# One driver for every seven-product unit, with weights prepared two pairs of products ahead

## The chip, the cores and the metric

One Trainium2 chip, one core. The metric is the device time of one execution in microseconds; the median of three runs is given, and one further execution is profiled. TensorE (PE) multiplies matrices, ScalarE (ACT) and VectorE (DVE) work elementwise, GpSimd (POOL) and SyncE (SP) mainly issue transfers here.

## The reference

One layer of a streaming encoder over 1024 tokens of width 1024, with 256 memory tokens, all in float32:

```python
h = rms_norm(x, g_mix)
c_h, c_b, c_c, sq, sk, sv, xq, gate_pre = split(h @ w_in)
y_conv = (c_b * causal_depthwise_conv(c_c * c_h, conv_w)) @ w_conv_out      # width 3
y_sb = stick_breaking_attention(heads(sq), heads(sk), heads(sv)) @ w_sb_out  # 16 heads of 64
mem_n = rms_norm(mem, g_mem)
y_x = memory_cross_attention(xq, mem_n, w_mem_kv, q_norm_g, k_norm_g) @ w_x_out  # 4 heads of 256
g = sigmoid(gate_pre)                                                        # one gate per branch
x = x + (g[0] * y_conv + g[1] * y_sb + g[2] * y_x) @ w_out
x = x + square(relu(rms_norm(x, g_mlp) @ w_up)) @ w_down                     # w_up 1024x4096
```

## The kernel before

TensorE multiplies fp32r operands. To keep float32 accuracy each operand is split in a rounded part (hi) and the rest (lo), and a product is three matmuls, hi*hi, hi*lo and lo*hi, for each of the pieces of 128 rows that it sums over. A *split* is one ACT instruction, which writes hi, and one DVE instruction behind it, which writes lo = source - hi (`split_o`).

Large products are done by a scheme that makes a 2x2 block product from seven half-size products instead of eight. One *unit* (class `Unit`) takes two column blocks of weights of 512 KB each (`load` fills `r1` and `r2`) and makes four 128x512 tiles per block pair. Its seven products are `p1` to `p7`; each is a `chain_mm` of twelve 128x512 matmuls into a PSUM bank. Its weights come in four steps: `w1` splits r1; `w2` and `w3` do two DVE subtractions or additions of half blocks and split the result; `w4` splits half of r2. `p1` and `p2` need w1, `p6` and `p5` need w2, `p7` and `p3` need w3, and `p4` needs w4. Bank `a` serves p1, p6, p7 and p4 one after the other, and is read out in between: after p1 into `x0`, after p6 into `xu` (ACT), after p7 (DVE), after p4 (ACT). A product that goes on in a bank waits for that reading. `fin` is what follows a unit.

The other operand are halves of the normed rows and their sums and differences, made once for a group of units by class `Seconds`: `first` makes those for p1 and p2; `second_a(rows, kk)`, for kk = 0 to 3, does eight transposes on TensorE, two evictions on ACT, four half-wide DVE instructions and a split, for p6 and p5; `second_b(kk)` does two splits, for p7, p3 and p4.

`drive(U, extra)` runs a list of units. It is called twice. *Drive 1* (from about 94 us to 373 us) has 13 units: four `QUnit`, and then three groups of an `HUnit`, a `CUnit` and a `BUnit`. The `fin` of a CUnit multiplies C by H on DVE and applies the three taps of the convolution: for each of two tiles one ACT instruction (the first tap) and two DVE instructions (the others). The `fin` of a BUnit multiplies the result by B and stores it. *Drive 2* (1625 us to 1957 us) has 16 `FUnit`, the w_up product. Between the drives stand the attention, the gates and the output products; behind drive 2 stands the w_down product, whose weights are fetched by `fetch(n)` and prepared by `prep(n, kp)`.

Ahead of drive 1, and before the change outside of it, eight products of the memory rows are made, `kv(0)` to `kv(7)`, 256 columns each, of 48 matmuls with 128x256 results; their weights come by `kv_load` and are split by `kv_split` (a CAST on ACT, a subtraction on DVE). kv(4) to kv(7) are interleaved with second_a(0) to second_a(3) of drive 1.

What sets the order: `act`, `vec` and the first matmul of each chain_mm are recorded by `keep_in_program_order`, so that these instructions stand on their engines as the code issues them; the other instructions are placed by a scheduler. Each engine works its row off in order. Pools give the buffers: 4 raw pages for loaded weights, 3 `whl` pages for split ones, 40 general pages, 3 pages for x0, and PSUM banks: 3 in `pd` (units' bank a), 2 in `pz`, 2 for transposes, 1 in `po`.

Of the kernel before, what the change touches and what calls it, by code (L numbers as in the profile page):

```python
# [42 lines left out]
def block_kernel(ctx, tc, x, mem, small, w_in, w_v, w_kv, w_co, w_so, w_xo, w_out, w_up, w_dn, out):  # L43
# [199 lines left out]

    def split_o(src, hi, lo):
        act(hi, src)
        vec(lo, src, ALU.subtract, f32v(hi))
# [13 lines left out]
    def chain_mm(ps, a, b, first=False, last=False):  # L260

        n = len(a)
        for i, ((ah, al), (bh, bl)) in enumerate(zip(a, b)):
            go = dict(skip_group_check=not first)
            m_ = nc.tensor.matmul(ps, lhsT=ah, rhs=bh, start=first and i == 0, stop=False, **go)  # L265
            if i == 0:
                order(m_)
            nc.tensor.matmul(ps, lhsT=ah, rhs=bl, start=False, stop=False, **go)  # L268
            nc.tensor.matmul(ps, lhsT=al, rhs=bh, start=False, stop=i == n - 1, **go)  # L269
# [52 lines left out]
    class Unit:  # L322
# [30 lines left out]

        def half(self):
            return hpp.tile([P, 512], F32, tag="hp", name=nm("xh"))

        def p1(self):
            self.a, self.x0 = pd(), self.half()
            chain_mm(self.a, col4(self.a11), self.h["11"], first=True)
            act(self.x0, self.a)  # L360
# [49 lines left out]
    def drive(U, extra):  # L410


        extra = iter(extra)

        def ex():
            next(extra, lambda: None)()

        NU = len(U)
        U[0].load()
        U[1].load()  # L420
        U[0].w1()
        U[1].w1()
        for u in range(2):
            ex()
            U[u].p1()
            ex()
            U[u].p2()
            U[u].w2()
        for u in range(2):
            ex()  # L430
            U[u].p6()
            ex()
            U[u].p5()
        for u in range(NU):
            un = U[u]
            nx = U[u + 1] if u + 1 < NU else None
            if u == 0:
                un.w3()
            if u < 2:
                un.w4()  # L440
            else:
                un.p1()
                U[u - 1].fin()
                un.w3()
                un.p2()
                un.w4()
            if u + 2 < NU:
                U[u + 2].load()
            if u >= 2:
                un.p6()  # L450
                un.p5()
            if u >= 1 and nx:
                nx.w1()
            un.p7()
            if u == 0:
                nx.w3()
            elif nx:
                nx.w2()
            un.p3()
            un.p4()  # L460
            if u == 0:
                un.fin()
        U[NU - 1].fin()
# [20 lines left out]
    def kv(cg):  # L484
# [3 lines left out]
        for i in range(NM):  # L488
            ps = pd()[:, 0:256]
# [51 lines left out]
    kv_load(5)  # L541
# [4 lines left out]
    for kk in range(4):  # L546
        kv_split(4 + kk)
        steps = kv(4 + kk)
        fill(steps, 4)
        if kk + 6 < 8:  # L550
            kv_load(kk + 6)
        sec_h.second_a(rows1, kk)
        run(steps)
    for i in range(NM):
        nc.gpsimd.dma_start(out=kv_scr[1][i], in_=vr[i])
    pin[0] = False
# [67 lines left out]
    drive(units, [lambda kk=kk: sec_h.second_b(kk) for kk in range(4)])  # L624
# [6 lines left out]
    for kk in range(4):  # L631
# [4 lines left out]
        split_o(h12[kk // 2][:, j * 512 : j * 512 + 512], *sec_h.h["12"][kk])  # L636

# [461 lines left out]
    class FUnit(Unit):  # L1099
# [36 lines left out]
    drive(  # L1136
        [FUnit(u) for u in range(16)],
        [lambda kk=kk: sec_f.second_a(late, kk) for kk in range(4)]
        + [lambda kk=kk: sec_f.second_b(kk) for kk in range(4)],
    )  # L1140
# [32 lines left out]
    def prep(n, kp):  # L1173
# [5 lines left out]
        t_ = tt.get((q, kp))  # L1179
        if j == 1:  # L1180
# [11 lines left out]
    fetch(0)  # L1192
    fetch(1)
    prep(0, 0)
    prep(0, 1)
# [84 lines left out]
```

## Time and profile before

| | before |
|---|---|
| median of 3 runs | 2268.62 us (2268.49 to 2269.18) |
| the profiled execution | 2269.87 us |
| its span | 2268.1 us |
| mean granted TensorE clock | 0.984 |
| DMA, mean over the span | 116 GB/s, 263.94 MB |

Rows of the timeline read: start and duration in us, engine, line of the code, operation, output<-input by the program's names, shape, how many instructions in a row are put together (x2), and in brackets the idle time of the engine ahead of it with what released it. In rows of time windows each engine has its busy time and, in parentheses, its number of instructions; behind them stand the granted clock (1 is full), the share of time in which the DMA engines were busy, and GB/s. Matmuls overlap, so the duration of one (0.39) is longer than the time from one start to the next (0.23). Names in capital L are lines: L236 is `act`, L233 is `vec`, L89 and L90 are the cast and the subtraction of the kv weights, L265, L268 and L269 the three matmuls of chain_mm, L203 to L205 those of kv, L603 the taps on DVE, L284 the eviction of transposes.

### The profile page before, as it was taken

How to read it: one execution, taken by the hardware profiler on the slowest of the kernel's cores; microseconds unless marked ns; L12 is line 12 of the kernel's file. 1: busy time of each engine (PE TensorE's matmuls, PEld its weight loads, DVE VectorE, ACT ScalarE, POOL GpSimd, SP SyncE). 2: the span in 40 equal slices, each digit the busy share in tenths (PEclk: the TensorE clock that was granted, in tenths of full speed). 3: DMA queues.
4: the chain of work that ended last, by engine and by line, in shares of the span. 5: the costliest groups of instructions: out<-in, count | busy, mean ns of one | idle time of the engine just before them, and what ended most of it. 6: DMA issues, size and time to landing. Idle time of an engine off the chain costs nothing.

```text
span 2268.1 us, 27004 instructions
## 1 busy us (share of the span) xinstructions
PE 2174.7 (96%) x10148; PEld 1800.8 (79%) x10148; DVE 1406.0 (62%) x1885; ACT 1004.3 (44%) x1791; POOL 385.1 (17%) x570
## 2 busy tenths in 40 slices
PE   6899998999999999999999999999989999999999
PEld 6778776888878778778788788888768888788887
DVE  4745555145688788787777534442565555677776
ACT  7522323235565565566555312111455555433332
POOL 1000000112333433433333000000111111100000
PEclk9999998999999999999999999999989999999999
DMA  5341224323222222222221445334134444744444
GB/s 205 130 130 56 75 74 162 94 88 112 84 75 66 84 80 69 75 84 65 75 93 66 140 142 163 105 100 151 68 120 154 152 150 152 264 174 135 153 149 139
DMA packets 74883, 263.94 MB, mean 116 GB/s; under 512 B 9728, under 2 KB 9728, under 8 KB 74752
## 3 DMA queue, kind: packets, MB, share of 16 engines
q1 hardware_dynamic: 53248, 188.27, 25.7%
q0 software_dynamic: 21504, 73.94, 8.7%
q8 instruction: 80, 1.31, 0.2%
q14 instruction: 51, 0.42, 0.1%
HBM read 179.86 MB, written 73.92 MB: 112 GB/s over the span
## 4 chain that ended last, share of the span: by engine, by line
PE 71%; DVE 10%; issue 7%; ACT 7%; POOL 4%; DMA 1%; POOLq 0%; DVEq 0%; ACTq 0%; SPq 0%
PE d L204 7%; PE d L205 6%; PE d L203 6%; PE d L269 6%; PE d L265 6%; PE d L268 6%; PE d L125 4%; PE d L126 4%; PE d L127 4%; PE z L265 4%; PE z L269 4%; PE z L268 4%; POOL pg L836 3%; DVE pg L233 2%; DVE pg L114 2%
## 5 line engine op out<-in xcount | busy, mean ns | idle before, releaser
L203 PE MATMUL d<-pg,whl 128*128 128x512 f32 x736 | 294.6, 400 | 0.3 <-ACT ox L744 0.3
L204 PE MATMUL d<-pg,whl 128*128 128x512 f32 x736 | 288.0, 391 | 0.0
L205 PE MATMUL d<-pg,whl 128*128 128x512 f32 x736 | 287.8, 391 | 0.0
L236 ACT ACTIVATE pg<-pg 128x512 f32<-128x512 f32 (+1 forms) x192 | 150.9, 791 | 305.6 <-DVE pg L233 303.6
L233 DVE TENSOR_TENSOR pg<-pg,pg 128x1024 fp32r<-128x1024 f32 (+3 forms) x180 | 184.7, 1032 | 72.2 <-ACT pg L236 70.4
L836 POOL TENSOR_SCALAR_AFFINE_SELECT pg<-pg 128x128 f32<-128x128 f32 x256 | 171.2, 675 | 279.6 <-ACT pg L833 269.2
L846 DVE TENSOR_TENSOR_SCAN pg<-pg,zero 128x128 f32<-128x128 f32 (+7 forms) x128 | 177.1, 1384 | 57.1 <-POOL pg L836 54.4
L265 PE MATMUL d<-pg,whl 128*128 128x512 f32 x444 | 179.6, 404 | 29.3 <-ACT pg L236 17.7
L113 ACT CAST pg<-t 128x256 fp32r<-128x256 f32 (+2 forms) x336 | 115.2, 368 | 203.0 <-DVE pg L114 145.4
L269 PE MATMUL d<-pg,whl 128*128 128x512 f32 x444 | 178.8, 403 | 2.5 <-DVE whl L233 2.4
L268 PE MATMUL d<-pg,whl 128*128 128x512 f32 x444 | 178.4, 402 | 1.2 <-DVE pg L233 1.2
L205 PEld LDWEIGHTS d<-pg,whl 128*128 128x128 f32 x736 | 138.2, 188 | 30.7
L203 PEld LDWEIGHTS d<-pg,whl 128*128 128x128 f32 x736 | 138.4, 188 | 25.8 <-ACT ox L744 1.1
L204 PEld LDWEIGHTS d<-pg,whl 128*128 128x128 f32 x736 | 138.6, 188 | 24.4
L265 PE MATMUL z<-pg,whl 128*128 128x512 f32 x396 | 154.9, 391 | 0.0
L269 PE MATMUL z<-pg,whl 128*128 128x512 f32 x396 | 154.6, 390 | 0.0
L268 PE MATMUL z<-pg,whl 128*128 128x512 f32 x396 | 154.6, 390 | 0.0
L125 PE MATMUL d<-pg,whl 128*128 128x512 f32 x384 | 150.7, 393 | 3.0 <-ACT whl L89 3.0
L89 ACT CAST whl<-raw 128x1024 fp32r<-128x1024 f32 x78 | 82.6, 1059 | 158.7 <-DMA raw<-in_w_co 62.8
L126 PE MATMUL d<-pg,whl 128*128 128x512 f32 x384 | 150.5, 392 | 0.0
L127 PE MATMUL d<-pg,whl 128*128 128x512 f32 x384 | 149.9, 391 | 0.0
L114 DVE TENSOR_TENSOR pg<-t,pg 128x256 fp32r<-128x256 f32 (+2 forms) x336 | 129.3, 404 | 30.5 <-ACT pg L113 27.1
(192 smaller groups left out, 4754.6 us busy)
## 6 DMA issues: line engine op xcount, KB each, us to landing
raw<-in_w_in SPq DMA_DIRECT2D x72, 512.0 KB, 3.6
raw<-in_w_up SPq DMA_DIRECT2D x32, 512.0 KB, 4.3
raw<-fscr_s SPq DMA_DIRECT2D x32, 512.0 KB, 3.7
pg<-in_w_dn SPq DMA_DIRECT2D x32, 512.0 KB, 4.9
gscr<-pg POOLq DMA_DIRECT2D x24, 512.0 KB, 2.9
raw<-gscr SPq DMA_DIRECT2D x24, 512.0 KB, 3.9
fscr<-pg POOLq DMA_DIRECT2D x48, 256.0 KB, 2.6
fscr_s<-pg POOLq DMA_DIRECT2D x48, 256.0 KB, 2.5
```

Of the source, the lines that this page charges most:

```text
L125: nc.tensor.matmul(ps, lhsT=ah, rhs=bh, start=i == 0, stop=False)
L126: nc.tensor.matmul(ps, lhsT=ah, rhs=bl, start=False, stop=False)
L127: nc.tensor.matmul(ps, lhsT=al, rhs=bh, start=False, stop=i == n - 1)
L203: nc.tensor.matmul(ps, lhsT=ah, rhs=bh, start=i == 0, stop=False)
L204: nc.tensor.matmul(ps, lhsT=ah, rhs=bl, start=False, stop=False)
L205: nc.tensor.matmul(ps, lhsT=al, rhs=bh, start=False, stop=i == n - 1)
L233: order(nc.vector.tensor_tensor(out=out, in0=a, in1=b, op=op))
L265: m_ = nc.tensor.matmul(ps, lhsT=ah, rhs=bh, start=first and i == 0, stop=False, **go)
L268: nc.tensor.matmul(ps, lhsT=ah, rhs=bl, start=False, stop=False, **go)
L269: nc.tensor.matmul(ps, lhsT=al, rhs=bh, start=False, stop=i == n - 1, **go)
L836: nc.gpsimd.affine_select(out=t_[:, W - P : W], in_=t_[:, W - P : W], pattern=[[-1, P]], compare_op=ALU.is_gt, fill=fill_, base=0, channel ...
L846: nc.vector.tensor_tensor_scan(out=rev, data0=rev, data1=zero.broadcast_to([P, W]), initial=1.0, op0=ALU.mult, op1=ALU.add)
```

## The change

1. `split_o` issues the DVE half of a split later: behind the next split's ACT half, or ahead of the next chain_mm (`owed`, `settle`).
2. `drive` goes through one list of pairs of products: (1, u) is p1 and p2 of unit u, (2, u) is p6 and p5, (3, u) is p7, p3 and then p4. It begins with (1,0) (1,1) (1,2) (1,3) (2,0) (2,1) (3,0) (3,1) (2,2) (3,2) (2,3) (3,3), and from unit 4 on has (1,u) (2,u) (3,u). Before, units 0 and 1 were interleaved, and from unit 2 on each went alone. Behind the first product of a pair the weights for the pair after the next are prepared. w4 and the load of unit u + 2 come in the pair ahead of (3, u). A unit's `fin` comes behind the second product of the next pair; before, it came behind p1 of the next unit, ahead of w3 and p2.
3. The four first units' r1 are loaded ahead, and once more by the later `load` (eight more loads of 512 KB in both drives). Unit 3 uses the bank of `po`.
4. In drive 1 kv(4) stays ahead of the drive; second_a(0) and kv(5), second_a(1), second_a(2) and kv(6), second_a(3), kv(7) are hooked in behind p2(0), p1(1), p2(1), p1(2), p2(2). The kv products use `pz` banks in place of `pd`. second_b(0) to (3) are hooked behind p6 and p5 of units 0 and 1.
5. In drive 2 second_a(0) to (3) come behind p2(0), p1(1), p2(1), p1(2), and second_b as in drive 1.
6. The last unit of drive 2 has the first fetches of w_down ahead of its p7, and the two first preparations ahead of its p3 and p4; before, all came behind the drive.

```diff
+    owed = []
+    def settle():
+        while owed:
+            lo, src, hi = owed.pop(0)
+            vec(lo, src, ALU.subtract, f32v(hi))
     def split_o(src, hi, lo):
         act(hi, src)
-        vec(lo, src, ALU.subtract, f32v(hi))
+        settle()
+        owed.append((lo, src, hi))
...
     def chain_mm(ps, a, b, first=False, last=False):
         n = len(a)
+        settle()
...
+        bank = staticmethod(pd)
         def p1(self):
-            self.a, self.x0 = pd(), self.half()
+            self.a, self.x0 = self.bank(), self.half()
...
-    def drive(U, extra):
+    def drive(U, hooks, late=None):
...
+        pairs = [(1, u) for u in range(4)] + [(2, 0), (2, 1), (3, 0), (3, 1)]
+        for u in range(2, NU):
+            pairs += [(k, u) for k in ((1, 2, 3) if u >= 4 else (2, 3))]
+        def prep(n):
+            if n < len(pairs):
+                k, u = pairs[n]
+                getattr(U[u], f"w{k}")()
+        for u in range(4):
+            U[u].r1 = load(U[u].s1_)
+        for n in range(2):
+            prep(n)
+        hook(-1, 0)
+        U[3].bank = po
+        done = None
+        for n, (k, u) in enumerate(pairs):
             un = U[u]
+            first, second = ((un.p1, un.p2), (un.p6, un.p5), (un.p7, un.p3))[k - 1]
+            final = n == len(pairs) - 1
+            if final and late:
+                late(0)
+            first()
+            prep(n + 2)
+            if n == 1:
+                U[0].load()
+            if n + 1 < len(pairs) and pairs[n + 1][0] == 3:
+                v = pairs[n + 1][1]
+                U[v].w4()
+                if v + 2 < NU:
+                    U[v + 2].load()
+            hook(n, 0)
+            if n == 2:
+                U[1].load()
+            if final and late:
+                late(1)
+            second()
+            if done:
+                done.fin()
+                done = None
+            hook(n, 1)
+            if k == 3:
+                if final and late:
+                    late(2)
+                un.p4()
+                done = un
+        done.fin()
...
-            ps = pd()[:, 0:256]
+            ps = pz()[:, 0:256]
...
-    for kk in range(4):
-        kv_split(4 + kk)
-        steps = kv(4 + kk)
-        fill(steps, 4)
-        if kk + 6 < 8:
-            kv_load(kk + 6)
-        sec_h.second_a(rows1, kk)
-        run(steps)
+    kv_split(4)
+    run(kv(4))
...
-    drive(units, [lambda kk=kk: sec_h.second_b(kk) for kk in range(4)])
+    hooks = {(-1, 0): lambda: kv_load(5), (0, 1): a_(0, 5), (1, 0): a_(1), (1, 1): a_(2, 6), (2, 0): a_(3), (2, 1): lambda: kv_late(7)}
+    hooks.update({(4 + kk // 2, kk % 2): b_(sec_h, kk) for kk in range(4)})
+    drive(units, hooks)
...
-    fetch(0)
-    fetch(1)
-    prep(0, 0)
-    prep(0, 1)
+    def ahead(i):
+        if i == 0:
+            fetch(0)
+            fetch(1)
+        else:
+            prep(0, i - 1)
+    drive([FUnit(u) for u in range(16)], hooks, ahead)
```

Three places show what this moves. The first is ACT's row where drive 1 begins. Before, around kv(4) and kv(5): whl_628 and pg_631 are kv(4)'s casts, t_666 and t_672 the transposes of second_a(0), pg_681 its split, whl_714 and pg_717 kv(5)'s casts.

```order
51 L89 CAST whl_628<-raw_504 128x1024
52 L89 CAST pg_631<-raw_506 128x1024
53 L284 ACTIVATE pg_664<-t_666,sm 128x512
54 L284 ACTIVATE pg_664<-t_672,sm 128x512
55 L236 ACTIVATE pg_681<-pg_665 128x1024
56 L499 COPY pg_626<-d_635 128x256
57 L499 COPY pg_627<-d_688 128x256
58 L89 CAST whl_714<-raw_592 128x1024
59 L89 CAST pg_717<-raw_594 128x1024
60 L284 ACTIVATE pg_750<-t_752,sm 128x512
```

After, around kv(5): xh_701 is the reading of p1(0), whl_716 the split of w1(2), t_736 and t_742 the transposes of second_a(0), pg_751 its split, whl_756 and pg_759 kv(5)'s casts, t_843 and t_849 the transposes of second_a(1).

```order
57 L236 ACTIVATE xh_701<-d_700 128x512
58 L236 ACTIVATE whl_716<-raw_687 128x1024
59 L296 ACTIVATE pg_734<-t_736,sm 128x512
60 L296 ACTIVATE pg_734<-t_742,sm 128x512
61 L236 ACTIVATE pg_751<-pg_735 128x1024
62 L89 CAST whl_756<-raw_696 128x1024
63 L89 CAST pg_759<-raw_698 128x1024
64 L296 ACTIVATE pg_841<-t_843,sm 128x512
65 L296 ACTIVATE pg_841<-t_849,sm 128x512
```

The casts of kv(5) stood ahead of the eviction of their neighbour's transposes, and stand now behind an eviction and a split that waits for DVE; a split of unit weights stands there too.

The second is ACT's row at the first B unit of drive 1, c = 2. Before: xh_1740 is the reading of p1 of that unit, the two rows with `sm` are the first taps, whl_1765 is w3's split, pg_1783 w4's, pg_1802<-d_1739 the reading of p6 for which p7 waits.

```order
137 L236 ACTIVATE xh_1740<-d_1739 128x512
138 L236 ACTIVATE pg_1533<-pg_1653,sm 128x1024
139 L236 ACTIVATE pg_1585<-pg_1705,sm 128x1024
140 L236 ACTIVATE whl_1765<-pg_1762 128x1024
141 L236 ACTIVATE pg_1783<-raw_1540 128x512
142 L236 ACTIVATE pg_1802<-d_1739 128x512
143 L236 ACTIVATE pg_1802<-z_1804 128x512
```

After: xh_1748 is that reading of p1, whl_1765 the split of w3, the rows with `sm` the taps, pg_1803<-d_1747 the reading of p6, whl_1805 the next unit's w1, pg_1807 w4's.

```order
137 L236 ACTIVATE xh_1748<-d_1747 128x512
138 L236 ACTIVATE whl_1765<-pg_1762 128x1024
139 L236 ACTIVATE pg_1539<-pg_1661,sm 128x1024
140 L236 ACTIVATE pg_1593<-pg_1713,sm 128x1024
141 L236 ACTIVATE pg_1803<-d_1747 128x512
142 L236 ACTIVATE whl_1805<-raw_1682 128x1024
143 L236 ACTIVATE pg_1807<-raw_1564 128x512
```

A split of the unit's weights moved from behind the taps to ahead of them; the taps are still ahead of the reading of p6, and w4's split moved behind it.

The third is ACT's row in drive 2 ahead of p7(0). Before: pg_13636 and the rows up to pg_13702 are the splits of second_b(0) to (3), with the readings of p6 and p5 of units 0 and 1 (sources d and z) among them.

```order
1358 L236 ACTIVATE pg_13626<-pg_13626 128x512 x2
1359 L236 ACTIVATE whl_13633<-pg_13630 128x1024
1360 L236 ACTIVATE pg_13636<-pg_13292 128x1024
1361 L236 ACTIVATE pg_13640<-pg_13472 128x512
1362 L236 ACTIVATE pg_13656<-d_13494 128x512
1363 L236 ACTIVATE pg_13658<-pg_13321 128x1024
1364 L236 ACTIVATE pg_13640<-pg_13509 128x512
1365 L236 ACTIVATE pg_13656<-z_13664 128x512
1366 L236 ACTIVATE pg_13678<-pg_13361 128x1024
1367 L236 ACTIVATE pg_13682<-pg_13554 128x512
1368 L236 ACTIVATE pg_13698<-d_13576 128x512
1369 L236 ACTIVATE pg_13700<-pg_13390 128x1024
```

After: xh_13685 is the reading of p1(3), whl_13702 the split of w2(1), the reading of d_13479 that of p6(0), whl_13739 w3(0), whl_13787 w3(1); the others from pg_13741 on are second_b(0) and (1) and the readings of p5(0) and p6(1).

```order
1362 L236 ACTIVATE xh_13685<-o_13684 128x512
1363 L236 ACTIVATE whl_13702<-pg_13699 128x1024
1364 L236 ACTIVATE pg_13718<-pg_13718 128x512 x2
1365 L236 ACTIVATE pg_13734<-d_13479 128x512
1366 L236 ACTIVATE whl_13739<-pg_13736 128x1024
1367 L236 ACTIVATE pg_13741<-pg_13300 128x1024
1368 L236 ACTIVATE pg_13745<-pg_13515 128x512
1369 L236 ACTIVATE pg_13734<-z_13749 128x512
1370 L236 ACTIVATE pg_13764<-pg_13329 128x1024
1371 L236 ACTIVATE pg_13745<-pg_13558 128x512
1372 L236 ACTIVATE pg_13782<-d_13536 128x512
1373 L236 ACTIVATE whl_13787<-pg_13784 128x1024
```

The splits of second_b now stand behind the splits of w2(1) and w3(0), where before w3(0) came behind all of them, and two units' p1 and p2 more stand ahead of them on TensorE.

More of the change, by code (lines that the diff above doesn't have):

```diff
@@ L408, in fin @@
             pass
-    def drive(U, extra):
-        extra = iter(extra)
-        def ex():
-            next(extra, lambda: None)()
+    def drive(U, hooks, late=None):
         NU = len(U)
[L419 to L434, printed above, removed]
-            un = U[u]
[L436 to L463, printed above, removed]
@@ new lines, in drive, with hook @@
+        pairs = [(1, u) for u in range(4)] + [(2, 0), (2, 1), (3, 0), (3, 1)]
[5 more added lines that the diff above has]
+                getattr(U[u], f"w{k}")()
+        def hook(n, i):
+            hooks.get((n, i), lambda: None)()
+        for u in range(4):
+            U[u].r1 = load(U[u].s1_)
+        for n in range(2):
+            prep(n)
@@ L540, in block_kernel @@
     run(kv(3))
-    kv_load(5)
     for i in range(NM):
@@ L545, in block_kernel, with kv_late @@
     vr = [page(F32) for _ in range(NM)]
-    for kk in range(4):
-        kv_split(4 + kk)
-        steps = kv(4 + kk)
-        fill(steps, 4)
-        if kk + 6 < 8:
-            kv_load(kk + 6)
-        sec_h.second_a(rows1, kk)
-        run(steps)
-    for i in range(NM):
-        nc.gpsimd.dma_start(out=kv_scr[1][i], in_=vr[i])
-    pin[0] = False
+    kv_split(4)
+    run(kv(4))
+    def kv_late(cg):
+        kv_split(cg)
+        if cg + 1 < 8:
+            kv_load(cg + 1)
+        run(kv(cg))
+        if cg == 7:
+            for i in range(NM):
+                nc.gpsimd.dma_start(out=kv_scr[1][i], in_=vr[i])
+            pin[0] = False
     class QUnit(Unit):
@@ L623, in block_kernel, with a_, go, b_ @@
         units += [hu, cu, BUnit(c, cu)]
-    drive(units, [lambda kk=kk: sec_h.second_b(kk) for kk in range(4)])
+    def a_(kk, cg=None):
+        def go():
+            sec_h.second_a(rows1, kk)
+            if cg:
+                kv_late(cg)
+        return go
+    def b_(sec, kk):
+        return lambda: sec.second_b(kk)
+    hooks = {(-1, 0): lambda: kv_load(5), (0, 1): a_(0, 5), (1, 0): a_(1), (1, 1): a_(2, 6), (2, 0): a_(3), (2, 1): lambda: kv_late(7)}
+    hooks.update({(4 + kk // 2, kk % 2): b_(sec_h, kk) for kk in range(4)})
+    drive(units, hooks)
     h12 = [load(t.rearrange("p a b -> p (a b)")) for t in h12_scr]
@@ L636, in block_kernel @@
         split_o(h12[kk // 2][:, j * 512 : j * 512 + 512], *sec_h.h["12"][kk])
+    settle()
     o_scr = [
@@ L1135, in block_kernel @@
     late = rows[4:8]
[L1136 to L1140, printed above, removed]
+    hooks = {
+        at: lambda kk=kk: sec_f.second_a(late, kk) for kk, at in enumerate(((0, 1), (1, 0), (1, 1), (2, 0)))
+    }
+    hooks.update({(4 + kk // 2, kk % 2): b_(sec_f, kk) for kk in range(4)})
     NAMES = ("11", "s1", "s2", "s4", "s3", "12", "22")
@@ L1179, in prep @@
         t_ = tt.get((q, kp))
+        settle()
         if j == 1:
```

## The prediction

> **What bounds the kernel now.** I read the page first, then the waits of TensorE, then the timeline of TensorE at each wait over half a microsecond, and at those places the rows of ScalarE (ACT) and VectorE (DVE). The page:
>
> ```profile
> PE 2174.7 (96%) x10148; PEld 1800.8 (79%) x10148; DVE 1406.0 (62%) x1885; ACT 1004.3 (44%) x1791; POOL 385.1 (17%) x570
> ...
> PEclk9999998999999999999999999999989999999999
> ```
>
> TensorE is busy 96% of the span. The change keeps its 9562 instructions, so a gain can come only from the 93 us of idle time and from stretches at a lower granted clock. Idle time of DVE and ACT is worth nothing in itself. Among the waits, those before the seven-product units are
>
> ```profile
> PE d L265 <- ACT pg L236: 17.7, 6, 4.5
> PE d L265 <- ACT whl L236: 11.5, 5, 4.4
> ```
>
> TensorE waits 29 us there, in eleven places (the columns are the sum, the count and the longest). With the lower clock behind them these are what the change can remove. Those of drive 1's start, with the four mem products ahead of them:
>
> ```profile
> 59.53 0.58 PE L204 MATMUL d<-whl,pg 128*128 128x256 f32 x1 [3.10 <-DVE whl L90]
> 66.90 0.28 PE L205 MATMUL d<-pg,pg 128*128 128x256 f32 x1
> 68.59 0.50 PE L203 MATMUL d<-whl,pg 128*128 128x256 f32 x2 [0.54 <-ACT whl L89]
> 69.85 0.39 PE L204 MATMUL d<-whl,pg 128*128 128x256 f32 x1 [0.76 <-DVE whl L90]
> 75.34 0.28 PE L205 MATMUL d<-pg,pg 128*128 128x256 f32 x1
> 93.92 0.50 PE L265 MATMUL d<-pg,whl 128*128 128x512 f32 x1 [1.42 <-ACT whl L236]
> 95.18 0.50 PE L269 MATMUL d<-pg,whl 128*128 128x512 f32 x1 [0.53 <-DVE whl L233]
> 112.16 0.50 PE L265 MATMUL d<-pg,whl 128*128 128x512 f32 x1 [0.81 <-ACT whl L236]
> 120.33 0.50 PE L265 MATMUL d<-pg,whl 128*128 128x512 f32 x1 [1.63 <-ACT whl L236]
> 121.59 0.61 PE L269 MATMUL d<-pg,whl 128*128 128x512 f32 x1 [0.53 <-DVE whl L233]
> 125.34 0.40 PE L269 MATMUL d<-pg,whl 128*128 128x512 f32 x1
> 141.91 0.39 PE L265 MATMUL z<-pg,whl 128*128 128x512 f32 x1
> 144.63 0.39 PE L265 MATMUL d<-pg,whl 128*128 128x512 f32 x1
> ```
>
> From 141.91 to 144.63 one product of twelve matmuls takes 2.72 us. The product that begins at 120.33 takes 5.24 (to 125.34 and one pitch), of which 0.53 is a wait: 2.0 go to a lower clock. Likewise the 256-wide product that was stopped for 3.10 takes 7.4 us from its third matmul on (59.53 to 66.90), the next one 5.5 (69.85 to 75.34): 1.9. So a stall of three microseconds costs its length and about 1.9 more.
>
> **The change, drive 1's start.** Before, the four last 256-wide mem products (kv) stand in a row, each with its casts ahead of the eviction of the sums; each costs 0.54 + 0.76 = 1.3 us of idle time. After, kv(5), (6) and (7) come behind a second product, and their casts stand behind the making of sums in ACT's queue. The durations:
>
> ```profile
> 67.49 1.05 ACT L89 CAST whl<-raw 128x1024 fp32r<-128x1024 f32 x1
> 68.57 1.23 DVE L90 TENSOR_TENSOR whl<-raw,whl 128x1024 fp32r<-128x1024 f32 x1 [3.00 <-ACT whl L89]
> 70.85 1.48 DVE L233 TENSOR_TENSOR pg<-pg,pg 128x512 f32<-128x512 f32 x2
> 72.36 1.06 ACT L236 ACTIVATE pg<-pg 128x1024 fp32r<-128x1024 f32 x1 [1.71 <-DVE pg L233]
> 74.60 0.69 DVE L233 TENSOR_TENSOR pg<-pg 128x512 f32<-128x512 f32 x1
> ```
>
> For kv(5): p2(0) ends; DVE takes its sum (0.69, as at 74.60), does the first two subtractions of second_a(0) (1.3), ACT splits their result (1.06), then casts (1.05): about 4.1 us. TensorE has eight transposes for 1.0 of it (from 66.90's end, 67.02, to 68.59 less its wait of 0.54). Idle 3.1, and 0.6 at the third matmul: 3.7 where it was 1.3. For kv(6) the same chain with the split of w1(3), 0.95, in the queue: 4.65. For kv(7) the cast needs a page that p2(2) reads until its end, and the subtraction then stands behind p2(2)'s sum and two more: 3.6. The weights of the first unit still wait for ACT, 2.0 (93.92 and 95.18: 1.95). Later the products p7(0) need the splits of second_b, which now come in a row with w3(0), w3(1) and w4(0): by the same durations p7(0) starts 3.35 late. The sum of idle time is 2.0 + 3.7 + 4.65 + 3.6 + 3.35 = 17.3. Now it is 1.95 + 3.9 + 1.34 (112.16, with 0.53 at its third matmul as at 121.59) + 2.16 (120.33, 121.59) = 9.35. Four of the new stalls are over three microseconds: at 1.9 for three and about 1 for the shorter train of p7(0) they cost 6.7 of clock, against 2.0 now. Loss: 17.3 - 9.35 + 6.7 - 2.0 = 12.7, say **13 us**. Bounds: +2 if only kv(5) stalls longer and no clock falls, +16 if all three mem products lose kv(6)'s 4.65 and the full 1.9.
>
> The eight more loads of 512 KB (the first weight of four units read twice) lie beside products while the DMA engines have room; SP has nothing queued behind them that is needed within a unit's 19 us. Costed at nothing; if that cover went, it would show as a DMA wait at p6(0).
>
> **C to B, three times.** Drive 1 ends with three groups of units H, C, B. Behind each C unit the taps are formed by DVE and ACT while TensorE runs the B unit:
>
> ```profile
> 218.27 0.60 ACT L236 ACTIVATE xh<-d 128x512 f32<-128x512 f32 x1 [2.12 <-PE d L269]
> 218.76 1.14 ACT L236 ACTIVATE pg<-pg,sm 128x1024 f32<-128x1024 f32 x1
> 219.94 2.60 DVE L603 SCALAR_TENSOR_TENSOR pg<-pg,sm,pg 128x1023 f32<-128x1023 f32 x2 [3.54 <-ACT pg L236]
> 220.56 0.39 PE L269 MATMUL z<-pg,whl 128*128 128x512 f32 x1
> 223.78 1.15 ACT L236 ACTIVATE pg<-pg,sm 128x1024 f32<-128x1024 f32 x1 [3.87 <-DVE pg L233]
> 228.80 1.06 ACT L236 ACTIVATE whl<-pg 128x1024 fp32r<-128x1024 f32 x1 [3.87 <-DVE pg L233]
> 230.28 0.58 ACT L236 ACTIVATE pg<-d 128x512 f32<-128x512 f32 x1
> 230.91 0.69 PE L265 MATMUL d<-pg,whl 128*128 128x512 f32 x1 [4.52 <-ACT pg L236]
> ```
>
> Let T0 be 220.56, the last matmul of p2. Two products later, at T0 + 5.67, p7 could start; it starts at T0 + 10.35, because ACT's queue has both taps, the split of w3 and only then the eviction of p6's bank (230.28). After, w3 is split ahead of the taps, but these begin only behind p2's sum: sum to T0 + 1.11, product 2.4, tap 3.66, two tap sums 6.2, second product 7.4, second tap 8.55, eviction 9.1, and p7 at T0 + 9.14. The delay falls from 4.68 to 3.5. The idle time is then 3.3, still over three, so I let the clock cost stay. Gain 3 x 1.2 = **3.6 us**. Bounds: nothing if the tap chain is 1.2 longer; 10 if the shorter wait no longer costs the clock (1.2 + 2.1 each).
>
> **End of drive 1.** ACT's order there is the same (the last eviction, four splits, the casts of the next stage): nothing.
>
> **Drive 2.** Its start today:
>
> ```profile
> 1625.20 2.35 DVE L233 TENSOR_TENSOR whl<-raw,whl 128x1024 fp32r<-128x1024 f32 x2
> 1649.46 0.79 PE L265 MATMUL d<-pg,whl 128*128 128x512 f32 x1 [2.96 <-ACT pg L236]
> 1665.90 0.79 PE L265 MATMUL d<-pg,whl 128*128 128x512 f32 x1 [4.44 <-ACT whl L236]
> 1671.55 0.39 PE L265 MATMUL z<-pg,whl 128*128 128x512 f32 x1
> ...
> 1625.00:1672.00 47.00, 36.35 (x136) 27.06 (x137) 34.13 (x44) 24.41 (x35) 1.13 (x2) 0.82 0.10 35
> ```
>
> p7(0) is complete at 1671.55, and 10.7 of those 47 us are idle. After, four more products (p1 and p2 of units 2 and 3, 10.9 us) come ahead of it, and TensorE reaches p7(0) without a long wait at 1663.2. But DVE must first have done 16 wide and 33 half-wide operations from 1625.20 on: 16 x 1.14 (the pitch in 1625.20's pair: 2.35 less 1.22) + 33 x 0.60 (74.60's 0.69 less the overlap of back-to-back instructions, 0.09 in that pair) = 38.0, to 1663.2 if it never waits. My ladder, with each wait for ACT's split in it, has the last sum's split at about 1670.5 and p7(0) complete at 1674. Less the four products that is 1663.1, against 1671.55: **8.5 us** gained. Bounds: DVE never waiting, p7(0) complete at 1665.9 and 16.5 gained; DVE busy at today's 34.13 of 47, the 38.0 take 52, p7(0) complete near 1678, 4.4 gained.
>
> Its end:
>
> ```profile
> 1957.00 0.50 PE L265 MATMUL d<-pg,whl 128*128 128x512 f32 x1 [3.24 <-ACT whl L236]
> 1958.45 0.80 PE L269 MATMUL d<-pg,whl 128*128 128x512 f32 x1 [0.63 <-DVE whl L233]
> 1969.90 1.22 DVE L233 TENSOR_TENSOR pg<-raw,pg 128x1024 fp32r<-128x1024 f32 x1
> ```
>
> The next stage's first weights are now prepared during the last unit, which takes away the 3.24. But its first product then waits at the seventh matmul for the second weight's split, and the products after it need the subtraction that ends at 1971.1 today. DVE has the same work before that one (the last unit's sums, the splits), so it ends no earlier; TensorE gets there sooner and waits there. Taken as **0**, between -3 and +1.5.
>
> **Sum.** 13 - 3.6 - 8.5 + 0 = +0.9. The profiled execution was 2269.87 (its span 2268.1 and 1.8 around it), 1.25 above the median of 2268.62; so 2270.8 in its terms, 2269.5 in the median's: 2270. A difference under 0.2%, 4.5 us, can hardly be told from none.
>
> **A rule weighed.** At 120.33 a wait of 1.63 and 0.53 already brought the lower clock, and at 1649.46 one of 2.96 made the next matmuls 0.79 long instead of 0.39. The Trainium skill, "TensorE: Matmul & The Clock Gate", section "What's actually happening", says the clock falls after an idle window of about 3.4 us and that the window runs free, so that the cost varies from run to run. By it, stalls of 3.1 to 3.35 us might cost no clock, and the sum would be the first rival's, 2258; the two rows disagree with it.
>
> **Rivals.** (1) The new stalls of 3.1 to 3.35 us cost no clock: drive 1 then loses 17.3 - 9.35 + 1.9 (kv(6)) - 2.0 = 8, C to B gains 10, drive 2 8.5: -10.5, 2258. For it, the window's position is unknown; against it, the three rows with shorter waits. Chance 0.1. (2) DVE hardly waits in drive 2: 16.5 gained there, -7, 2261. For it, the sums come two pairs ahead; against it, each split crosses from DVE to ACT and back. Chance 0.2. (3) The other side: DVE's queue at the second sums is the bound at both starts. Drive 1 loses 16 and drive 2 gains 4.4, with the C to B gain unchanged or gone: +8 to +11.6, 2277 to 2280. It decides where p7(0) of drive 2 is complete after 1676. For it, DVE is only 73% busy there today because it waits for ACT. Chance 0.22. (4) The change does nothing at C to B, since ACT still has both taps ahead of the eviction: +4.5, 2273. Chance 0.1, on the border. The forecast itself: 0.38.
>
> **Chances and range.** Faster: rivals 1 and 2, 0.30. Slower: rival 3 and most of 4, 0.29. Same: 0.41. The range goes from rival 1's 2258 to rival 3's 2280; the forecast's own is 2265 to 2275.
>
> **What would show it.** In the profile after: waits of 3 to 4.7 us before three 256-wide products between 75 and 120 us, released by ACT's cast or DVE's subtraction, with the granted clock low in those stretches; p7 of the B units released by ACT after about 3.3 us instead of 4.5; one long wait, 6 to 9 us, at p7(0) of drive 2 and none at 1649; no 3.24 us wait at the change to the last stage but one some 13 us on. The prediction is wrong if the mem products wait about a microsecond (faster by ten), or if a seven-product unit in the middle of a drive gets a wait that I worked out as hidden (each 0.5 us of it costs 12 in 25 of the 29 units).

## The result, and the profile after

The changed kernel takes 2279.3 us (median of 4 runs, 2277.87 to 2280.34), the kernel before 2268.9 (4 runs, 2268.49 to 2269.55). The ratio is 1.0045, with a 95% interval of 1.0028 to 1.0063: slower by about 10 us. The profiled execution took 2278.89, its span is 2277.2, so 9.1 more than before.

The first lines of the profile's page, with busy time per engine, and the granted TensorE clock in 40 slices:

```profile
PE 2180.7 (96%) x10148; PEld 1804.3 (79%) x10148; DVE 1405.6 (62%) x1885; ACT 1004.0 (44%) x1791; POOL 384.1 (17%) x570
...
PEclk9899999999999999999999999999999999999999
```

TensorE has 6.0 us more of busy time with the same instructions, so they ran at a lower clock in places, and 3.1 us more of idle time; where, the page doesn't tell. So I cut both timelines of TensorE at five points that both programs have, and compared the lengths. The points are the third matmul of kv(4), the start of the wait at p7 of the first B unit, the first product behind drive 1, p1(0) of drive 2 and p4(15) of drive 2. A forecast is given where the prediction had one:

| stretch | before | after | difference | forecast |
|---|---|---|---|---|
| to kv(4) | 59.53 | 58.42 | -1.1 | - |
| kv(4) to the first B unit's p7 | 166.9 | 180.0 | +13.1 | +13 |
| to the end of drive 1 | 147.0 | 142.3 | -4.7 | -3.6 |
| to drive 2 | 1252.1 | 1251.0 | -1.1 | - |
| p1(0) to p4(15) of drive 2 | 325.3 | 318.3 | -7.0 | -8.5 |
| p4(15) to the end | 317.2 | 327.2 | **+10.0** | **0** |

The stalls of drive 1's start, on TensorE:

```profile
58.42 0.58 PE L204 MATMUL z<-whl,pg 128*128 128x256 f32 x1 [2.79 <-DVE whl L90]
67.92 0.50 PE L277 MATMUL d<-pg,whl 128*128 128x512 f32 x1 [1.42 <-ACT whl L236]
78.67 0.80 PE L203 MATMUL z<-whl,pg 128*128 128x256 f32 x2 [3.33 <-ACT whl L89]
99.57 0.79 PE L203 MATMUL z<-whl,pg 128*128 128x256 f32 x2 [4.08 <-ACT whl L89]
114.89 0.38 PE L203 MATMUL z<-whl,pg 128*128 128x256 f32 x1 [1.13 <-ACT whl L89]
116.87 0.38 PE L203 MATMUL z<-whl,pg 128*128 128x256 f32 x1 [1.60 <-DVE pg L233]
118.00 0.39 PE L204 MATMUL z<-whl,pg 128*128 128x256 f32 x1 [0.75 <-DVE whl L90]
143.63 0.50 PE L277 MATMUL d<-pg,whl 128*128 128x512 f32 x1 [0.64 <-ACT pg L236]
145.16 0.50 PE L280 MATMUL d<-pg,whl 128*128 128x512 f32 x1 [1.03 <-DVE pg L233]
```

The releasers at 78.67 and 99.57 are the casts (L89) of kv(5) and kv(6), and the first matmuls behind are 0.80 long where those at 67.92 are 0.50: the clock is low. The three B units' p7, and the products of drive 2's start:

```profile
241.53 0.80 PE L277 MATMUL d<-pg,whl 128*128 128x512 f32 x1 [3.16 <-ACT pg L236]
303.56 0.80 PE L277 MATMUL d<-pg,whl 128*128 128x512 f32 x1 [3.16 <-ACT pg L236]
366.91 0.50 PE L277 MATMUL d<-pg,whl 128*128 128x512 f32 x1 [3.17 <-ACT pg L236]
...
1631.67 0.50 PE L277 MATMUL d<-pg,whl 128*128 128x512 f32 x1 [2.30 <-ACT whl L236]
1673.38 0.50 PE L280 MATMUL d<-pg,whl 128*128 128x512 f32 x1 [0.76 <-DVE pg L233]
1677.74 0.80 PE L277 MATMUL d<-pg,whl 128*128 128x512 f32 x1 [3.62 <-ACT pg L236]
```

Then the change to the last stage. A column there is four products that share their weights. TensorE no longer waits before the stage's first matmul, but at its seventh, and then 6.19 us at the seventh of the second column. The first three rows are from after:

```profile
1956.80 0.50 PE L277 MATMUL d<-pg,pg 128*128 128x512 f32 x1 [2.52 <-ACT pg L236]
1976.70 0.79 PE L277 MATMUL z<-pg,pg 128*128 128x512 f32 x1 [6.19 <-ACT pg L236]
1978.74 0.80 PE L281 MATMUL z<-pg,pg 128*128 128x512 f32 x1 [0.82 <-DVE pg L233]
...
1970.47 0.39 PE L265 MATMUL z<-pg,whl 128*128 128x512 f32 x1
1971.83 0.39 PE L265 MATMUL z<-pg,pg 128*128 128x512 f32 x1
```

The last two rows are from before, the first and the seventh matmul of the second column: neither waits. VectorE's row and GpSimd's of after tell why:

```profile
1967.16 0.69 DVE L233 TENSOR_TENSOR pg<-d,pg 128x512 f32<-128x512 f32 x1 [2.95 <-DMA pg<-xscr]
1972.79 0.69 DVE L233 TENSOR_TENSOR pg<-d,pg 128x512 f32<-128x512 f32 x1 [3.80 <-DMA pg<-xscr]
1975.73 1.22 DVE L233 TENSOR_TENSOR pg<-pg,pg 128x1024 fp32r<-128x1024 f32 x1 [1.12 <-ACT pg L236]
...
1977.48 1.22 DVE L233 TENSOR_TENSOR pg<-raw,pg 128x1024 fp32r<-128x1024 f32 x1
...
1964.29 0.53 POOL L1233 DMA_DIRECT2D pg<-xscr  x1 [1.66 <-DMA fscr<-pg]
1967.59 0.53 POOL L1233 DMA_DIRECT2D pg<-xscr  x1 [2.78 <-PE o L280]
1970.10 0.53 POOL L1233 DMA_DIRECT2D pg<-xscr  x1 [1.98 <-DMA fscr_s<-pg]
```

The first column's sums are added to pages of the residual (x_scr), which eight transfers load. In the kernel before, GpSimd issued seven of them in one go (the last column is how many), and VectorE did its first two additions without a wait:

```profile
1957.05 3.69 POOL L1198 DMA_DIRECT2D pg<-xscr  x7
1965.21 1.28 DVE L233 TENSOR_TENSOR pg<-d,pg 128x512 f32<-128x512 f32 x2
```

After, the preparations that part 6 moved ahead have taken general pages, and the loads wait one by one for pages that the last unit's stores (fscr) and TensorE still read. VectorE stands 2.95 and 3.80 us at additions for which the residual has not come, and behind them in its row stands the work for the second column, whose last subtraction (1977.48) ends at 1978.7 where it ended at 1971.1 before. The Trainium skill, "PSUM — Partial Sum Buffer", section "Engine vs sequencer instructions", says that the queues of ScalarE, VectorE and GpSimd are strictly first in, first out; these rows agree with it.

### The profile page after: what moved, and what is told of

It is laid out like the page before. It is cut to its first block, busy times and chain, and to the rows that moved or that the text cites. A ratio compares the mean times of both kernels' runs of the same rounds, so it can differ in the third digit from the quotient of the medians.

```text
span 2277.2 us, 27042 instructions
## 1 busy us (share of the span) xinstructions
PE 2180.7 (96%) x10148; PEld 1804.3 (79%) x10148; DVE 1405.6 (62%) x1885; ACT 1004.0 (44%) x1791; POOL 384.1 (17%) x570
## 4 chain that ended last, share of the span: by engine, by line
PE 57%; issue 20%; DVE 9%; POOL 7%; ACT 6%; DMA 1%; POOLq 0%; DVEq 0%; ACTq 0%; SPq 0%
PE d L204 5%; PE d L203 5%; PE d L205 5%; PE d L125 4%; PE d L126 4%; PE d L127 4%; PE d L281 4%; PE d L277 4%; PE d L280 4%; POOL pg L866 3%; PE z L281 2%; PE z L277 2%; PE z L280 2%; DVE pg L114 2%; POOL fscr_s L1163 1%
## 5 line engine op out<-in xcount | busy, mean ns | idle before, releaser
L203 PE MATMUL d<-pg,whl 128*128 128x512 f32 x736 | 294.5, 400 | 0.3 <-ACT ox L774 0.3
L204 PE MATMUL d<-pg,whl 128*128 128x512 f32 x736 | 287.8, 391 | 0.0
L205 PE MATMUL d<-pg,whl 128*128 128x512 f32 x736 | 287.8, 391 | 0.0
L277 PE MATMUL d<-pg,whl 128*128 128x512 f32 x420 | 168.7, 402 | 17.5 <-ACT pg L236 13.8
L280 PE MATMUL d<-pg,whl 128*128 128x512 f32 x420 | 168.0, 400 | 3.3 <-DVE pg L233 3.2
L281 PE MATMUL d<-pg,whl 128*128 128x512 f32 x420 | 167.5, 399 | 1.2 <-DVE whl L233 1.0
L125 PE MATMUL d<-pg,whl 128*128 128x512 f32 x384 | 150.6, 392 | 3.2 <-ACT whl L89 3.2
L89 ACT CAST whl<-raw 128x1024 fp32r<-128x1024 f32 x78 | 82.5, 1057 | 159.5 <-DMA raw<-in_w_co 53.1
L126 PE MATMUL d<-pg,whl 128*128 128x512 f32 x384 | 150.3, 392 | 0.0
L233 DVE TENSOR_TENSOR whl<-pg,whl 128x1024 fp32r<-128x1024 f32 x58 | 71.1, 1226 | 127.9 <-ACT whl L236 127.9
L127 PE MATMUL d<-pg,whl 128*128 128x512 f32 x384 | 149.9, 391 | 0.0
```

What stands on the lines that cost most here:

```text
L125: nc.tensor.matmul(ps, lhsT=ah, rhs=bh, start=i == 0, stop=False)
L203: nc.tensor.matmul(ps, lhsT=ah, rhs=bh, start=i == 0, stop=False)
L233: order(nc.vector.tensor_tensor(out=out, in0=a, in1=b, op=op))
```

## The experiments

The kernel before ran beside each group; its medians there were 2269.0 to 2269.8.

**Part 6 undone.**

```diff
-    drive([FUnit(u) for u in range(16)], hooks, ahead)
+    drive([FUnit(u) for u in range(16)], hooks)
+    for i in range(3):
+        ahead(i)
```

> Undoes part 6 alone: the first fetches and preparations of the last stage come behind drive 2 again, everything else as after. Theory T (the last stage's additions wait for the loads of the residual pages, which come late because the early preparations hold the pages; the subtractions for the second column stand behind those additions): the 6.19 us wait before the second column goes, the 3.2 us wait before the first comes back, and the time falls by 7 to 9 us from after's 2279.3, to 2271. Rival U (the second column waits for its own work on DVE and ACT, whatever the pages): the wait at the first column comes back and that at the second shrinks by no more than that, within 2 us of 2279.

Measured: 2268.29 us, 11.0 less than after; against before 0.9999 (0.9990 to 1.0009). The wait at the second column is gone, that at the first is back:

```profile
1952.67 0.50 PE L277 MATMUL d<-pg,whl 128*128 128x512 f32 x1 [3.24 <-ACT whl L236]
```

So the stage's own work was not late, as rival U had it. From p4(15) to the end this trace takes 318.8 us, 8.4 less than after, which is within the 7 to 9 that was expected. The rest of the 11.0 lies in stretches in which the two programs are the same (the table at the end of this section).

**The residual loaded ahead of the fetches.**

```diff
         if i == 0:
+            for t in range(8):
+                acc[t] = page(F32)
+                nc.gpsimd.dma_start(out=acc[t], in_=x_scr[t])
             fetch(0)
             fetch(1)
...
-    for t in range(8):
-        acc[t] = page(F32)
-        nc.gpsimd.dma_start(out=acc[t], in_=x_scr[t])
```

> As after, but the eight loads of the residual pages are issued at the start of the last unit, ahead of the first fetches, so that they have their pages before the preparations. Theory T: VectorE no longer waits for these loads, the wait of 6.19 us before the second column falls below 1.5, and the time to about 2270 (9 us less). Rival U: the wait stays above 4 us and the time within 2 us of 2279.

Measured: 2274.9 us, 4.4 less than after (1.0024 of before, 1.0015 to 1.0034). The wait of 6.19 us shrank to 1.24, as theory T has it, but the time fell by half of what it said. The first preparation now waits for its own block, which is transferred beside 4 MB of residual. ACT's row:

```profile
1951.97 1.06 ACT L236 ACTIVATE pg<-pg 128x1024 fp32r<-128x1024 f32 x1 [3.60 <-DMA pg<-in_w_dn]
```

**The residual loaded in unit 13.**

```diff
+    def residual():
+        for t in range(8):
+            acc[t] = page(F32)
+            nc.gpsimd.dma_start(out=acc[t], in_=x_scr[t])
+    hooks[(41, 1)] = residual
...
-    for t in range(8):
-        acc[t] = page(F32)
-        nc.gpsimd.dma_start(out=acc[t], in_=x_scr[t])
```

> As after, with the eight loads of the residual pages issued behind the second product of a pair of unit 13, some 30 us ahead of the first fetches of the last stage, so that they neither wait for pages nor share the DMA engines with those fetches. In the run with the loads just ahead of the fetches the wait at the second column was gone, but the first preparation waited 3.60 us for its fetched block. Theory T: both waits go, time 2266 to 2270. Rival: 40 pages are too few for eight more over two units; then waits come in units 14 and 15 and the time stays above 2274.

Measured: 2275.73 us (1.0026, 1.0016 to 1.0036). Both waits for transfers are gone (0.79 us is left at the second column), but two waits come near the end of the drive that after hasn't, where the rival expected them:

```profile
1926.23 0.50 PE L277 MATMUL d<-pg,whl 128*128 128x512 f32 x1 [0.85 <-ACT pg L236]
1942.11 0.50 PE L277 MATMUL d<-pg,whl 128*128 128x512 f32 x1 [1.98 <-ACT xh L236]
1961.53 0.50 PE L277 MATMUL d<-pg,pg 128*128 128x512 f32 x1 [2.52 <-ACT pg L236]
```

The wait at the seventh matmul stays (the last row). From p4(15) to the end the trace takes 319.7 us, 7.5 less than after and near the 318.8 of the run without part 6. So the loads' lateness is the cause of the 6.19 us and of most of what the last stage lost. The gain is spent earlier: from p1(0) to p4(15) it takes 321.1, where the runs beside it take 316.0. The first of the two new waits is one for a page, as the rival has it. ACT's reading of p6, for which p7 waits, is held up by a store from a page (fscr<-pg). The reading takes its input from TensorE's bank, so what it needs of the store is the page, to write into:

```profile
1925.58 0.60 ACT L236 ACTIVATE pg<-d 128x512 f32<-128x512 f32 x1 [3.58 <-DMA fscr<-pg]
```

The second new wait was not followed to its page. Neither of the two places tried for the loads was free of cost.

**The sums made ahead of drive 1 (part 4 undone, but for second_b's place).**

```diff
-            ps = pz()[:, 0:256]
+            ps = pd()[:, 0:256]
...
+    kv_load(5)
...
-    kv_split(4)
-    run(kv(4))
+    for kk in range(4):
+        kv_split(4 + kk)
+        steps = kv(4 + kk)
+        fill(steps, 4)
+        if kk + 6 < 8:
+            kv_load(kk + 6)
+        sec_h.second_a(rows1, kk)
+        run(steps)
...
-    hooks = {(-1, 0): lambda: kv_load(5), (0, 1): a_(0, 5), (1, 0): a_(1), (1, 1): a_(2, 6), (2, 0): a_(3), (2, 1): lambda: kv_late(7)}
+    hooks = {}
```

> Undoes part 4 alone: kv(4) to kv(7) and second_a(0) to (3) stand interleaved ahead of drive 1 as before, second_b stays hooked; the rest as after. By the accounting of the two traces drive 1's start lost 12.1 us, of which some 7 are idle time at the three mem products and the rest the lower clock behind them. Expected: 10 to 12 us less than after, 2268 to 2269, with waits of about 1.3 us at each mem product and no clock below 0.95 there. Rival: the loss is in the late splits at p7(0), which stay; then 2274 or more.

Measured: 2262.59 us, 16.7 less than after and 0.9971 (0.9959 to 0.9982) of before. The fall is more than the 10 to 12 that was expected. From kv(4) to the first B unit this trace takes 164.3 us: 15.6 less than after, and 2.5 less than before. So making the sums inside the drive (the weave) loses about 16 here, not 13. The waits at 112.16 and 120.33 of before, which the prediction lists, are gone by the new order of units, in which p1 and p2 of four units stand ahead of p6. Beside the old waits of kv and w1 only these are left, at p7(0):

```profile
127.78 0.51 PE L277 MATMUL d<-pg,whl 128*128 128x512 f32 x1 [0.70 <-ACT pg L236]
129.32 0.68 PE L280 MATMUL d<-pg,whl 128*128 128x512 f32 x1 [1.03 <-DVE pg L233]
```

How much the order is worth by itself stays open: the run "Both undone" below has the same program there and takes 166.9, as long as before.

**The mem products in a row, the sums woven.** The same loop without its line second_a, and second_a(0) to (3) hooked in as in after.

> As after, but kv(4) to kv(7) are done in a row ahead of drive 1, without the sums between them; second_a(0) to (3) stay hooked into the drive. Theory K (the loss at drive 1's start lies in the casts of kv that stand behind a sum's split): no wait over 1.4 us before a 256-wide product, and the time falls by 9 to 13 us from after's 2279.3, to 2266 to 2270. Rival S (the making of the sums inside the drive is itself what costs, as VectorE falls behind): waits of 3 us and more appear at p7(0) as in drive 2, and the gain is under 6 us.

Measured: 2275.25 us, 4.0 less than after (1.0029, 1.0019 to 1.0038). The mem products' waits fall to 1.41 and 0.76, as theory K says, but the loss turns up where rival S puts it, at p7(0):

```profile
139.74 0.79 PE L277 MATMUL d<-pg,whl 128*128 128x512 f32 x1 [3.69 <-ACT pg L236]
141.27 0.80 PE L280 MATMUL d<-pg,whl 128*128 128x512 f32 x1 [0.74 <-DVE pg L233]
```

It is like the wait at drive 2's p7(0) (3.62 and 0.73). So the casts behind the splits were only the first place at which VectorE's and ACT's work for the sums came out; with the sums woven in, it comes out at one place or the other.

**Both undone.**

> Undoes parts 4 and 6 (sums made ahead of drive 1, last stage prepared behind drive 2), keeps the order of units, the place of the ends, the deferral and drive 2's weaving. If the two losses are independent: 2279.3 - 16.7 - 11.0 = 2251.6, about 17 below before. If they share anything (a later place in the program, the clock's window), 2255 to 2260.

Measured: 2254.25 us (0.9933, 0.9916 to 0.9949), 25.0 less than after where the two alone sum to 27.7. They are nearly independent. The rest of the change (order, deferral, place of the ends, drive 2's weave) is worth 15 us against before.

**The ends of units behind the first product.** The two lines `if done: done.fin(); done = None` move from behind `second()` to behind `prep(n + 2)`.

> As after, but a unit's end comes behind the first product of the next pair (as before the change) and not behind the second, still with the next weights split ahead of it. The taps then start 2.72 us earlier on VectorE against TensorE's products; the wait before p7 of the three B units should fall from 3.16 to below 1.2 us and cost no clock: 3 x (2 to 4) = 6 to 12 us less than after, 2267 to 2273. Rival: the sum of p2 behind the taps holds up the next product in its bank, and the gain is under 3 us.

Measured: 2279.01 us (1.0043, 1.0028 to 1.0058): nothing. The wait moved from p7's first matmul to its third:

```profile
242.85 0.50 PE L281 MATMUL d<-pg,whl 128*128 128x512 f32 x1 [2.56 <-DVE whl L233]
```

It is the subtraction of w3's split: the deferral puts it behind the taps. With `settle()` ahead of `done.fin()`:

> As after, with a unit's end behind the first product of the next pair as in the run before, and now the outstanding subtraction of w3's split issued ahead of it. In the run before, p7's first matmul no longer waited but its third did, 2.56 us, for that subtraction, which the deferral had put behind the taps. Theory D (the deferral spoils it): the waits at p7 of the three B units fall below 1.2 us in sum each and cost no clock; 7 to 12 us less than after, 2267 to 2272. Rival P (p2's sum, then p6's reading, are held up by the taps whatever the split): a wait above 2 us stays at p7 or comes at p5, and the gain is under 3 us.

Measured: 2276.19 us (1.0032, 1.0021 to 1.0043), 3.1 less than after; the interval overlaps that of after, so this run alone does not show the gain. A wait of 2.56 us stays, at p7's first matmul, now for the reading of p6 by ACT: theory D explained one wait, and P's stood right behind it. Both undone as well:

> Parts 4 and 6 undone and the ends behind the first product with the split's subtraction ahead: the sum of the runs above. If all are independent and theory D holds: 2251.6 - 8 = 2243 to 2246; if the ends bring nothing, 2251 to 2253.

Measured: 2250.45 us (0.9917, 0.9902 to 0.9932). The ends bring 3.8, and here no execution is as slow as the fastest with both undone (2252.76). From the first B unit's p7 to the end of drive 1 it takes 137.9 us, as in the run before, where with both undone it takes 140.9.

**The taps of the second tile behind the reading of p6.** `fin` of a CUnit does tile 0; tile 1 follows behind the first product of the pair after.

> The kernel of 2250.45 us with the taps of the second tile issued one pair later, behind the reading of p6, so that the reading for which p7 waits stands behind one tap only. Theory P: the three waits of 2.56 us at p7 of the B units go, and the time falls by 7 to 9 us to 2242 to 2244. Rival: the second tile's taps then hold up p7's sum and p3's, and a wait of 2 us comes one product later; 2249 to 2251.

Measured: 2246.0 us (0.9900, 0.9885 to 0.9915), 4.4 less, between the two expectations. p7's wait is gone, as theory P has it; smaller ones came one product and two products later, where the rival expected one of 2 us:

```profile
226.64 0.50 PE L277 MATMUL z<-pg,whl 128*128 128x512 f32 x1 [0.95 <-ACT pg L236]
230.62 0.50 PE L277 MATMUL d<-pg,pg 128*128 128x512 f32 x1 [0.95 <-DVE pg L233]
```

This is the fastest version: 1.0% under before.

**The deferral (part 1) taken out** of the kernel of 2250.45 us: `split_o` issues its subtraction at once.

> The kernel of 2250.45 us (three parts mended) with the subtraction of each split issued at once again, that is without part 1. If the deferral matters to nothing there: within 1.5 us of 2250.5. If it keeps VectorE from standing at the wait for ScalarE where two splits follow each other (second_b, the splits of the last stage): 2 to 6 us slower, at p7(0) of both drives.

Measured: 2255.66 us (0.9939, 0.9927 to 0.9952), 5.2 slower. The new waits are in drive 2's start, not at p7(0) but ahead of it, in the products between the sums:

```profile
1642.39 0.50 PE L280 MATMUL d<-pg,whl 128*128 128x512 f32 x1 [0.53 <-DVE whl L233]
1644.81 0.49 PE L276 MATMUL d<-pg,whl 128*128 128x512 f32 x1 [0.53 <-ACT pg L236]
1647.87 0.80 PE L276 MATMUL z<-pg,whl 128*128 128x512 f32 x1 [1.07 <-DVE pg L233]
```

From p1(0) to p4(15) it takes 322.8 us, 4.1 more than the kernel of 2250.45 and 2.5 less than before. So much of drive 2's gain comes from the deferral, which the forecast had not given a price of its own.

**The additions of the first column last**, in the kernel of 2246.0 us with part 6 put back:

```diff
-            vec(acc[t0 + i][:, s], banks[i], ALU.add, acc[t0 + i][:, s])
+            for m in () if n == 0 and i < 3 else range(4) if n == 0 else (i,):
+                vec(acc[t0 + m][:, s], banks[m], ALU.add, acc[t0 + m][:, s])
```

> The kernel of 2246.0 us with part 6 as in after again (first fetches and preparations of the last stage inside the last unit), and the four additions of the first column moved behind both preparations of the second column in VectorE's row; the loads of the residual pages stay as late as in after. Part 6 alone cost 11 us. Theory T (the second column's weights stood behind additions that wait for late loads): no wait over 1.5 us before the second column, and within 2 us of 2246. Rival U (these preparations are late by themselves, through pages or transfers): the wait of 4 to 6 us stays and the time is 2254 or more.

Measured: 2256.36 us (0.9941, 0.9923 to 0.9959), 10.4 more than without part 6. Theory T's number is missed, and the time is the one that rival U gave, though not by U's way. The wait at the second column is gone, as T has it; it came back one column later, since the additions still wait for the loads and now stand ahead of the third column's work:

```profile
1951.78 0.69 DVE L233 TENSOR_TENSOR pg<-d,pg 128x512 f32<-128x512 f32 x1 [3.52 <-DMA pg<-xscr]
1954.65 0.69 DVE L233 TENSOR_TENSOR pg<-d,pg 128x512 f32<-128x512 f32 x1 [2.18 <-DMA pg<-xscr]
...
1960.17 0.49 PE L277 MATMUL d<-pg,whl 128*128 128x512 f32 x1 [1.59 <-ACT whl L236]
1962.22 0.80 PE L281 MATMUL d<-pg,whl 128*128 128x512 f32 x1 [1.24 <-DVE whl L233]
1965.99 0.80 PE L277 MATMUL d<-pg,pg 128*128 128x512 f32 x1 [1.69 <-ACT pg L236]
```

**The stretches in the other traces**, cut at the same five points:

| kernel | kv(4) to the first B unit's p7 | to the end of drive 1 | p1(0) to p4(15) | p4(15) to the end |
|---|---|---|---|---|
| before | 166.9 | 147.0 | 325.3 | 317.2 |
| after | 180.0 | 142.3 | 318.3 | 327.2 |
| part 6 undone | 181.1 | 141.3 | 316.0 | 318.8 |
| residual ahead of the fetches | 183.9 | 140.9 | 316.0 | 322.9 |
| residual in unit 13 | 184.2 | 140.9 | 321.1 | 319.7 |
| sums ahead of drive 1 | 164.3 | 142.2 | 316.0 | 328.0 |
| both undone | 166.9 | 140.9 | 316.1 | 319.9 |

Up to the end of drive 1 the four kernels from after to "residual in unit 13" run the same program. Their waits in the first of these stretches add up to 16.2 to 16.6 us, yet its length differs by 4.2: the rest is matmuls at a lower clock. So one trace tells the length of a stretch with such waits to some 4 us only, and there is one trace of before.

## Why the prediction was right or wrong

The forecast was 2270 and no clear difference; measured was 2279.3, slower, at the upper end of the range. One step failed, drive 2's end, and it makes the difference; the errors of the other steps nearly cancel in the profiled execution.

- **Drive 1's start, 13 us lost: right in kind; that it came to 13.1 is luck.** The waits were 3.33 + 0.46, 4.08 + 0.47 and 3.5 at the three mem products where 3.7, 4.65 and 3.6 stood, and 2.1 at p7(0) where 3.35 stood; with the first unit's 1.95 that is 15.9 where 17.3 stood. The lower clock was put 4.7 above that of before. In after it cost some 6.5 more (13.1 less the 6.6 of waits), and in the three other traces of the same program the stretch lost 14.2, 17.0 and 17.3 with nearly the same waits. So the waits were sized a little too large and the clock too small.
- **C to B, 3.6 us gained: right in kind**, 4.7 for the rest of drive 1 (4.7 to 6.2 in the traces of the table). The wait is 3.16 where 3.3 was worked out, released by ACT as stated. The taps ahead of the reading in ACT's row, to which the fourth rival pointed, did not take the gain away, but they held the rest of the wait: placed in two, they gave 4.4 more.
- **Drive 2's start, 8.5 us gained: right in kind**, 7.0 up to the last unit. p7(0) was complete at 1682.0, or 1675.9 when counted from before's start of drive 2, where 1674 stood. In five other traces of the same start (the runs of the table) it comes 1.6 us sooner, at 1674.3. The one long wait was 3.62 with smaller ones around it, not 6 to 9.
- **Drive 2's end, taken as 0 between -3 and +1.5: wrong**, +10.0. With part 6 undone the same stretch takes 8.4 less, so that much is part 6. The step says that "DVE has the same work before that one, so it ends no earlier". It counted VectorE's work and not what this work waits for. The additions in that row need the residual pages, and their loads need pages that part 6 had given to the preparations; the subtraction for the second column ended at 1978.7 and not at 1971.1, 7.6 later, and behind the wait the granted clock was 0.50 (1976 to 1981). I had the order of VectorE's row, and did not follow each operand of the additions back to its load and the load to its page.
- The third rival gave 2277 to 2280, the measured time, by another way: it had drive 1 lose 16 and drive 2 gain 4.4, and nothing at drive 2's end. In after drive 1 lost 13.1 and drive 2 gained 7.0, and 10 us of the loss came at the end, so the number agreed by chance. Its mechanism isn't refuted: p7(0) was complete a tenth of a microsecond ahead of the mark that it set, and the run with the mem products in a row shows VectorE's and ACT's work for the sums as the bound at drive 1's start.
- The loads read twice cost nothing that shows. No wait of TensorE in either drive names a load. VectorE does wait for one in drive 1, 4.57 us, ahead of the second unit's w2:

```profile
123.66 0.69 DVE L233 TENSOR_TENSOR pg<-raw 128x512 f32<-128x512 f32 x1 [4.57 <-DMA raw<-in_w_in]
```

  The next waits of TensorE, 0.64 and 1.03 at p7(0), are 0.70 and 1.03 in the run with the sums ahead, where VectorE has no such wait.
- A count in the prediction is wrong: the profile's page gives 10148 instructions of TensorE, before and after, not 9562. Nothing in the sum rests on it.

## What to carry to other kernels

Work moved ahead takes its buffers along: before preparing a stage early, list which later loads lived on the pages that it will hold, and who stands behind those loads' users in an in-order row. An engine that makes operands for two purposes is late at the first product whose operand stands last in its row; moving that product only shows the next one, so weave work in only as fast as the slower of the two engines can make it. Undo one part of a large change at a time: here two of six parts lost 25 us and hid a version 0.7% faster than before.

## What the runs showed of the hardware

The same wait did not cost the same clock. In the kernel with both parts undone, the three B units each wait 3.16 us at p7, and the granted clock (the column behind the five engines) in the five microseconds behind is 1.00, 0.50 and 0.66:

```profile
227.00:232.00 5.00, 4.08 (x18) 3.39 (x19) 4.55 (x5) 2.82 (x5) 0.00 (x0) 1.00 0.00 0
288.00:293.00 5.00, 4.50 (x11) 3.55 (x12) 4.30 (x4) 2.40 (x4) 0.00 (x0) 0.50 0.00 0
351.00:356.00 5.00, 4.15 (x11) 3.30 (x12) 3.17 (x3) 1.80 (x4) 0.00 (x0) 0.66 0.06 4
```

The starts of p7 are 60.58 and 63.35 us apart there; 21 products of 2.72 (57.1) and the wait of 3.16 make 60.3, so the clock cost 0.3 the first time and 3.1 the second, where I had put 1.9 on most stalls. The Trainium skill, "TensorE: Matmul & The Clock Gate", section "What's actually happening", says that the window runs free and that the point at which the clock changes depends on where in the window the first matmul lands. The three rows agree with a cost that varies; that the window is its cause no row shows. The same section of the Trainium skill gives an idle window of about 3.4 us as the condition of the lower clock; with that the rows do not agree, since waits of 3.16 brought it twice of three times.
